# Where the projection's block products stand between the attention's transposes, and how the final rows are grouped for the way out

## The chip, the cores and the metric

The kernel runs on one core of one Trainium2 chip. The metric is the device time of one execution in microseconds (us). Before the change it is 2482.18 us, the median of three runs from 2481.7 to 2482.43 us. The engines are named as in the profile: PE is TensorE's matmul, PEld its weight load, DVE is VectorE, ACT is ScalarE, POOL is GpSimd, SP is SyncE, which issues most DMAs.

## The reference

Two layers of a streaming encoder, for 512 new frames of one stream and 16 frames of each of 8 running streams (640 token columns), with the same weights. Each layer is a half-step SwiGLU block, a mixer and a second half-step SwiGLU block; a last RMSNorm ends it.

```python
for l in range(DEPTH):                                   # DEPTH = 2, D_MODEL = 1024, D_FF = 2816
    x = x + 0.5 * _swiglu(_rmsnorm(x, norm_ffn1[l]), w_ffn1_gu[l], w_ffn1_down[l])
    z = _rmsnorm(x, norm_mix[l]) @ w_in[l]               # conv B, C, V | q | k | v | gates
    y_conv = B * causal_depthwise_conv3(C * V)
    y_attn = chunk_band_attention(q, k, v, rel_bias[l])  # 8 heads x 64, scores + bias, softmax, p @ v
    m = g_conv * (y_conv @ w_conv_out) + g_attn * (y_attn @ w_attn_out)
    x = x + m @ w_o
    x = x + 0.5 * _swiglu(_rmsnorm(x, norm_ffn2[l]), w_ffn2_gu[l], w_ffn2_down[l])
y = _rmsnorm(x, norm_final)
```

All is in float32. The outputs are y, the new k and v rows and the new convolution rows.

## The kernel before

The state x lies in SBUF as `xall`, 128 partitions by 8 row blocks by 640 columns; `x[k]` is one row block. Every operand of a matmul is kept as a high part and a low part (`whi`, `wlo`, `hhim`, `hlom`, `thi`, `tlo`), so a product is three matmuls. Weights come in slabs of 128x1024: SP loads `raw`, ACT makes `whi` of it (L305), DVE makes `wlo` (L310).

**The mixer's products.** A pair of projection blocks is computed by `seven` (L818), a generator that makes seven block products in 14 steps and writes three PSUM tiles, `ma`, `mb` and `mc`. One step is six matmuls of 128x320 (L395). The steps of one product family come in the order X11, X21 (into `ma`, `mb`), N6 (onto `ma`), T5 (into `mc`), T7 (onto `ma`), 22 (onto `mc`), T4 (onto `ma`), two steps each. Between them PSUM tiles are read: ACT copies `ma` after X11 (L836) and after N6 (L844), and `mc` after T5 (L848, into the tile `c`); the product 22 adds onto `mc`, so it may start only when that copy has been made.

**The attention.** `fill(n)` (L1736) takes the next n steps from one stream of such families. Their PE work is laid between the steps of the attention, on which PE would otherwise wait. Two heads make a pair, and each layer has four pairs. For a pair, `scores(p)` computes scores of 128 queries at a time, DVE adds the bias and takes the maximum, ACT does the exponentials (L1969) and the scaling (L1816). `values(p)` then works in three pieces, divided by `yield`. The first piece transposes the weights of the key blocks j = 0 and 1 for both heads on PE (14 transposes, L1829), into four PSUM tiles `ptp`. The second transposes those of j = 2 and 3 (6 transposes). The third is the product with the values (`py`, L1843) and its copy by ACT (L1845). L1832 copies each `ptp` to SBUF (`pt`): DVE does six of a pair's eight, ACT does two, those of the second head with j = 1 and j = 3. The pool `att` has four PSUM banks, so the transposes of the second piece reuse the banks of the first piece, each after its copy.

On PE the order of the program is kept there (`manual_schedule` with PE alone); DVE and ACT are ordered by a scheduler that follows the program's order with some instructions given priority (`soon()`).

**The end.** `Final.all` (L2018) makes the last down projection in two parts of the columns: part A is the first 384 and part B is the last 256. While PE computes part B's row blocks m = 0 to 7, part A's statistics are finished and its rows are scaled and sent: `two(k, rr)` (L2110) multiplies two row blocks of A by their norm on DVE (L2112, 128x768) and SP issues one DMA for them (L2113). This happens after the row blocks m = 5, 6 and 7 of part B, and once more after part B's norm has been made diagonal by `turn(1)`. Then PE spreads part B's norm (`nbcf`, L2103), and `out` (L2115) scales part B's eight row blocks on DVE (L2116), each sent by its own DMA, in turn from SP and ACT (L2118).

Of the kernel before, what the change touches and what calls it, by code (L numbers as in the profile page):

```python
# [13 lines left out]
ALU = mybir.AluOpType  # L14
PSUM = bass.MemoryType.PSUM

P = 128
# [30 lines left out]
PARTS = slice(0, 3 * P), slice(3 * P, T)  # L48
# [132 lines left out]
def trunk(ctx: ExitStack, tc: tile.TileContext, xin, xtok, wst, small, pbias, samplebias, kcache, vcache,  # L181
          yout, ko, vo, co):
    nc = tc.nc
    PE, DVE, ACT, POOL, SP = nc.tensor, nc.vector, nc.scalar, nc.gpsimd, nc.sync
# [21 lines left out]
    def acc(name):  # L206
        return banks["acc"].tile([P, 2, 512], F32, tag="acc", name=name)

    def att(name):
        return banks["att"].tile([P, 512], F32, tag="att", name=name)  # L210
# [15 lines left out]
    for kind, inside in kinds():  # L226
        n = len(fourth)
# [20 lines left out]
    def add(out, a, b):  # L248
        DVE.tensor_tensor(out=out, in0=a, in1=b, op=ALU.add)  # L249
# [58 lines left out]
    def flush():  # L308
        for lo, src, hi in pending:
            DVE.tensor_tensor(out=lo, in0=src, in1=hi.bitcast(F32), op=ALU.subtract)  # L310
        pending.clear()
# [97 lines left out]
    def stir(ps, n):  # L409
        for _ in range(n):  # L410
            PE.matmul(ps[:, :P], ones, ones, start=True, stop=True)
# [4 lines left out]
    xall = xp.tile([P, KT, T], F32, name="x")  # L416
# [75 lines left out]
    def scaled(out, ps, rr):  # L492
        DVE.tensor_tensor(out=halves(out), in0=two(ps), in1=halves(rr), op=ALU.mult)
# [121 lines left out]
    def opening(fp, name, goff, n, put, tails):  # L615
# [45 lines left out]
        def out(i):  # L661

            j, up = divmod(i, 2)
            if not up:
                gs.append(tmp(f"g{name}_{j}"))
                if j:
                    scaled(gs[j], ps[i], ex.rho)
                    ACT.activation(gs[j], gs[j], AF.Silu)
                else:
                    ACT.copy(halves(gs[j]), two(ps[i]))  # L670
                return
            u = tmp(f"u{name}_{j}") if j > 1 else fp.tile([P, T], F32, tag="cap", name=f"u{name}_{j}", bufs=5)
            us.append(u)
            if j:
                scaled(u, ps[i], ex.rho)
                DVE.tensor_tensor(out=u, in0=u, in1=gs[j], op=ALU.mult)
            else:
                ACT.copy(halves(u), two(ps[i]))
# [559 lines left out]
    def mixer(l, after):  # L1238
        with tc.tile_pool(name=f"yp{l}", bufs=1, reuse_waits="tile") as yp, \
# [19 lines left out]
            with tc.tile_pool(name=f"mp{l}", bufs=2, reuse_waits="tile") as mp:  # L1259
# [63 lines left out]
                with tc.manual_schedule(engines={mybir.EngineType.PE}):  # L1323
                    attention(l, h, st, stats, ops, mp, yas, ycp, both, others())
# [374 lines left out]
    def attention(l, h, norms, stats, ops, mp, yas, ycp, both, others):  # L1699


        rr = norms.rr
# [33 lines left out]
        def fill(n):  # L1736
            for _ in range(n):
                next(stream, None)
# [80 lines left out]
        def values(p):  # L1819

            pt = [mp.tile([P, offs[-1] + SEQ], F32, name=f"pt{l}_{2 * p + e}", tag="pt") for e in range(2)]
            at = [sum(P * (NQ - i) for i in range(j)) for j in range(NQ)]

            def turn(j, e):
                w = (NQ - j) * P
                s = weights[2 * p + e]
                ptp = att(f"ptp{l}_{2 * p + e}_{j}")[:, :w]
                for i in range(j, NQ):
                    PE.transpose(ptp[:, (i - j) * P : (i - j + 1) * P],  # L1829
                                 s[:, offs[i] + j * P : offs[i] + (j + 1) * P], ident)  # L1830
                with soon():
                    (ACT.copy if e and j % 2 else DVE.tensor_copy)(pt[e][:, at[j] : at[j] + w], ptp)  # L1832

            for j in range(NQ):
                for e in range(2):
                    turn(j, e)
                if j % 2:
                    yield
            py = att(f"py{l}_{p}")
            for j in range(NQ):  # L1840
                for e in range(2):
                    hh = 2 * p + e
                    PE.matmul(py[e * HD : (e + 1) * HD, j * P :], vs[j][:, hh * HD : (hh + 1) * HD],  # L1843
                              pt[e][:, at[j] : at[j] + (NQ - j) * P], start=j == 0, stop=j == NQ - 1)
            ACT.copy(yas[:, p, 0:SEQ], py)  # L1845
            yield
# [5 lines left out]
        for p in range(npair):  # L1852
            if p + 1 < npair:
                scores(p + 1)
                fill(4)
            vals = values(p)
            next(vals)
            fill(3)
            next(vals)
            fill(2)  # L1860
            next(vals)
            fill(5)


        sbias = mp.tile([P, KS], F32, name=f"sbias{l}", bufs=1)
# [143 lines left out]
    class Final:  # L2009
# [8 lines left out]
        def all(self, ops):  # L2018
            ws = [[tiles.take() for _ in ops] for m in range(KT)]
            flush()  # L2020
            rr = pool[0].tile([P, PARTS[0].stop], F32, tag="even", name="frr", bufs=1)
            A, B = PARTS

            ACT.activation(early, x[KT - 1][:, 0:1], AF.Sqrt, bias=epst[:, 0:1], scale=0.0)
            for m in range(KT):
                self.product(0, m, ops, ws[m])
                self.take(0, m, m < KT - 1)
                if m:
                    self.scale(m - 1)
            for m in range(KT):  # L2030
                self.product(1, m, ops, ws[m])
                if m == 2:
                    self.ps = att("npsf0")[:, : A.stop // P]
                    for b in range(A.stop // P):
                        PE.matmul(self.ps[:, b : b + 1], self.ssum[0][:, b * P : (b + 1) * P], ones[:, 0:1],
                                  start=True, stop=True)
                    self.root(0)
                if m == 3:
                    self.turn(0)
                    self.scale(KT - 1)  # L2040
                if m == 4:
                    ps = self.spread(0)
                if m == 5:
                    self.ps = acc("npsf1")[:, :, 0]
                    self.idle = acc("stirf")[:, 0]
                    self.add(self.ssum[1], True)
                if m > 4:
                    self.add(self.sq)
                if m == 0:
                    last = self.sq  # L2050
                self.take(1, m, m < 4)
                if m == 0:
                    add(self.ssum[0], self.ssum[0], last)
                if m == 4:
                    ACT.copy(rr, ps)
                if m > 4:
                    self.two(2 * m - 10, rr)
            stir(self.idle, 3)
            self.add(self.sq, False, True)
            stir(self.idle, 5)  # L2060
            self.root(1)
            self.turn(1)
            self.two(6, rr)
            ps = self.spread(1)
            for k in range(KT):
                self.out(k, B, ps)
# [40 lines left out]
            xk = x[k][:, PARTS[0]]  # L2107
            ACT.activation(xk, xk, AF.Copy, scale=sm[:, O_GF + k : O_GF + k + 1])

        def two(self, k, rr):  # L2110
            z = xall[:, k : k + 2, PARTS[0]]
            DVE.tensor_tensor(out=z, in0=z, in1=rr.unsqueeze(1).to_broadcast([P, 2, rr.shape[1]]), op=ALU.mult)  # L2112
            SP.dma_start(yout[:, k : k + 2, PARTS[0]], z)  # L2113

        def out(self, k, c, ps):  # L2115
            DVE.scalar_tensor_tensor(out=x[k][:, c], in0=x[k][:, c], scalar=sm[:, O_GF + k : O_GF + k + 1],  # L2116
# [167 lines left out]
```

## Time and profile before

| what | value |
|---|---|
| time, median of three runs | 2482.18 us (2481.7 to 2482.43) |
| the profiled execution's own time | 2482.18 us |
| its span | 2480.2 us |
| PE busy | 2469.0 us, 100% of the span |
| DVE busy | 2119.5 us, 85% |
| ACT busy | 1442.9 us, 58% |
| POOL busy | 361.1 us, 15% |
| granted clock of TensorE | 0.999 |
| moved from and to HBM | 223.75 MB read, 7.94 MB written |

The page gives each engine's busy time, the chain of work that ended last, and groups of instructions. A row of the timeline is start, duration (both us), engine, line, operation, output<-inputs, and in brackets the idle time of that engine just before the instruction and what ended it. A matmul's row is longer than its turn on PE, because matmuls are pipelined: the turn is read from the starts of two rows that follow each other. In the row of a wait the total, the number of times and the longest are given.

### The profile page before, as it was taken

Reading aid. Unit: us, or ns where it says so; the run is one execution under the profiler, and the core shown is the slowest. Engines: PE = TensorE matmul, PEld = TensorE weight load, DVE = VectorE, ACT = ScalarE, POOL = GpSimd, SP = SyncE. Lnnn points to the kernel's source line nnn. Section 1 sums busy time; section 2 is a strip of 40 time slices with the busy share of each in tenths; the row PEclk is TensorE's granted clock in tenths of the full one; section 3 lists DMA queues with packets and bytes.
Section 4 is the critical chain, followed back from the end, with each engine's and each line's share of the span. In section 5 each row is a group of like instructions: output and inputs, shape, how many; then the busy total and the mean of one; then the engine's idle time right before and its main releaser. Section 6 shows DMA issues by size and latency. Waiting matters only on the chain.

```text
span 2480.2 us, 43569 instructions
## 1 busy us (share of the span) xinstructions
PE 2469.0 (100%) x17070; PEld 2422.0 (98%) x17070; DVE 2119.5 (85%) x3344; ACT 1442.9 (58%) x2337; POOL 361.1 (15%) x445
## 2 busy tenths in 40 slices
PE   9999999999999999999999999999999999999998
PEld 9999999889999999999999999998899999999998
DVE  7789888878888899888798889888788888989887
ACT  6445556665666555555565555556656665555555
POOL 0011211210111011111001111221101210111111
PEclk9999999999999999999999999999999999999999
DMA  5245665335345345555435454643344553555554
GB/s 189 82 115 125 136 136 130 107 111 175 104 112 153 95 117 121 133 136 136 117 92 129 129 132 123 138 120 110 122 156 123 119 140 92 122 131 124 129 136 111
DMA packets 134925, 310.72 MB, mean 125 GB/s; under 512 B 12896, under 2 KB 76768, under 8 KB 134720
## 3 DMA queue, kind: packets, MB, share of 16 engines
q1 hardware_dynamic: 70640, 221.80, 27.2%
q0 software_dynamic: 63360, 85.50, 20.7%
q8 instruction: 133, 2.18, 0.4%
q10 hardware_dynamic: 720, 0.65, 0.1%
q14 instruction: 72, 0.59, 0.1%
HBM read 223.75 MB, written 7.94 MB: 93 GB/s over the span
## 4 chain that ended last, share of the span: by engine, by line
PE 96%; ACT 2%; DVE 1%; DMA 0%; issue 0%; DVEq 0%
PE pab L395 12%; PE paa L395 11%; PE pcb L395 6%; PE pca L395 6%; PE dab L1086 5%; PE daa L1086 5%; PE qa L395 4%; PE po L372 4%; PE pbb L395 3%; PE pba L395 3%; PE dcb L1086 3%; PE dca L1086 3%; PE pda L372 2%; PE pv L1752 2%; PE poa L372 2%; PE ma_cv L395 2%
## 5 line engine op out<-in xcount | busy, mean ns | idle before, releaser
L310 DVE TENSOR_TENSOR wlo<-raw,whi 128x1024 fp32r<-128x1024 f32 (+1 forms) x582 | 597.4, 1030 | 243.2 <-ACT whi L305 240.1
L305 ACT CAST whi<-raw 128x1024 fp32r<-128x1024 f32 (+1 forms) x582 | 520.3, 896 | 359.2 <-PE pbb L395 39.4
L305 ACT CAST whi<-s 128x1024 fp32r<-128x1024 f32 (+1 forms) x164 | 153.4, 936 | 243.9 <-issue 109.1
L395 PE MATMUL pab<-xhib,whi 128*128 128x320 f32 x704 | 217.8, 309 | 0.0
L395 PE MATMUL pab<-xlob,whi 128*128 128x320 f32 x704 | 217.4, 309 | 0.0
L395 PE MATMUL pab<-xhib,wlo 128*128 128x320 f32 x704 | 217.4, 309 | 0.0
L395 PE MATMUL paa<-xhia,whi 128*128 128x320 f32 x640 | 197.9, 309 | 0.0
L395 PE MATMUL paa<-xhia,wlo 128*128 128x320 f32 x640 | 197.7, 309 | 0.0
L395 PE MATMUL paa<-xloa,whi 128*128 128x320 f32 x640 | 197.7, 309 | 0.0
L310 DVE TENSOR_TENSOR wlo<-s,whi 128x1024 fp32r<-128x1024 f32 (+1 forms) x164 | 176.3, 1075 | 6.4 <-ACT whi L305 6.1
L395 PEld LDWEIGHTS pab<-xhib,whi 128*128 128x128 f32 x704 | 132.2, 188 | 0.2
L395 PEld LDWEIGHTS pab<-xlob,whi 128*128 128x128 f32 x704 | 132.2, 188 | 0.2
L395 PEld LDWEIGHTS pab<-xhib,wlo 128*128 128x128 f32 x704 | 132.2, 188 | 0.0
L395 PEld LDWEIGHTS paa<-xloa,whi 128*128 128x128 f32 x640 | 120.2, 188 | 0.1
L395 PEld LDWEIGHTS paa<-xhia,whi 128*128 128x128 f32 x640 | 120.2, 188 | 0.1
L395 PEld LDWEIGHTS paa<-xhia,wlo 128*128 128x128 f32 x640 | 120.2, 188 | 0.0
L249 DVE TENSOR_TENSOR raw<-raw,raw 128x512 f32<-128x512 f32 x164 | 112.0, 683 | 1.2
L249 DVE TENSOR_TENSOR raw<-s,raw 128x512 f32<-128x512 f32 x164 | 111.9, 682 | 0.0
L395 PE MATMUL pcb<-xhib,whi 128*128 128x320 f32 x352 | 108.9, 309 | 0.0
L395 PE MATMUL pcb<-xlob,whi 128*128 128x320 f32 x352 | 108.7, 309 | 0.0
L395 PE MATMUL pcb<-xhib,wlo 128*128 128x320 f32 x352 | 108.7, 309 | 0.0
L1110 POOL DMA_DIRECT2D x<-c_b x52 | 62.6, 1203 | 310.4 <-ACT c_b L1103 104.1
(852 smaller groups left out, 8144.9 us busy)
## 6 DMA issues: line engine op xcount, KB each, us to landing
raw<-in_wst SPq DMA_DIRECT2D x374, 512.0 KB, 3.6
x<-c_b POOLq DMA_DIRECT2D x52, 320.0 KB, 5.1
x<-c_a POOLq DMA_DIRECT2D x50, 320.0 KB, 5.0
kc<-in_kcache SPq DMA_DIRECT2D x32, 256.0 KB, 3.7
vc<-in_vcache SPq DMA_DIRECT2D x16, 512.0 KB, 5.5
ub<-cbb POOLq DMA_DIRECT2D x42, 160.0 KB, 5.9
ua<-cba POOLq DMA_DIRECT2D x38, 160.0 KB, 5.5
x<-u_a POOLq DMA_DIRECT2D x18, 320.0 KB, 5.1
```

Of the source, the lines that this page charges most:

```text
L249: DVE.tensor_tensor(out=out, in0=a, in1=b, op=ALU.add)
L305: ACT.copy(hi[:, d], src[:, c])
L310: DVE.tensor_tensor(out=lo, in0=src, in1=hi.bitcast(F32), op=ALU.subtract)
L372: PE.matmul(ps[a] if isinstance(ps, list) else ps[:, a, :HT], w, x[:, a * HT : (a + 1) * HT], start=first and j == 0, stop=last and j == 2)
L395: PE.matmul(ps, a, b, start=start and kp == 0 and j == 0, stop=stop and kp == NP - 1 and j == 2, skip_group_check=True)
L1086: PE.matmul(ps[u], w, y, start=start and i == 0 and j == 0, stop=i == 1 and j == 2, skip_group_check=True)
L1110: POOL.dma_start(rows(r, cols), z, accum_op=ALU.add)
L1752: PE.matmul(pv[t], xx[:, t * P : (t + 1) * P], w[:, kk * AW : (kk + 1) * AW], start=c == 0 and kk == 0 and j == 0, stop=c == KT // 2 - 1 a ...
```

## The change

In the attention, after a pair's first piece of transposes two steps are filled in where there were three, and behind the values six where there were five; two stay between the second transposes and the values. The number of steps for a pair, ten here, is unchanged. At the end, part A's eight row blocks go out in groups of 3, 1, 3 and 1 where they went as four pairs; the number of DMAs stays four.

```diff
             vals = values(p)
             next(vals)
-            fill(3)
+            fill(2)
             next(vals)
             fill(2)
             next(vals)
-            fill(5)
+            fill(6)
...
                 if m > 4:
-                    self.two(2 * m - 10, rr)
+                    self.rows(*((0, 3), (3, 1), (4, 3))[m - 5], rr)
             stir(self.idle, 3)
             self.add(self.sq, False, True)
             stir(self.idle, 5)
             self.root(1)
             self.turn(1)
-            self.two(6, rr)
+            self.rows(7, 1, rr)
             ps = self.spread(1)
...
-        def two(self, k, rr):
-            z = xall[:, k : k + 2, PARTS[0]]
-            DVE.tensor_tensor(out=z, in0=z, in1=rr.unsqueeze(1).to_broadcast([P, 2, rr.shape[1]]), op=ALU.mult)
-            SP.dma_start(yout[:, k : k + 2, PARTS[0]], z)
+        def rows(self, k, n, rr):
+            z = xall[:, k : k + n, PARTS[0]]
+            DVE.tensor_tensor(out=z, in0=z, in1=rr.unsqueeze(1).to_broadcast([P, n, rr.shape[1]]), op=ALU.mult)
+            SP.dma_start(yout[:, k : k + n, PARTS[0]], z)
```

PE's order at the first head pair of the first layer, as the difference of the two programs. `ptp_0_2` is the transpose for head 0 and key block 2; the rows with `mc_qk` ahead of it are the last of the product T5, and those with `ma_qk` are the product T7.

```order
 L395 MATMUL mc_qk_5382<-hhim_6_4655,wlo_5234 128x320
+L1829 MATMUL ptp_0_2_5395<-ident,yc_4689 128x128 x2
+L1829 MATMUL ptp_1_2_5399<-ident,yc_4689 128x128 x2
+L1829 MATMUL ptp_0_3_5403<-ident,yc_4689 128x128
+L1829 MATMUL ptp_1_3_5406<-ident,yc_4689 128x128
 L395 MATMUL ma_qk_5261<-thi_0_4690,whi_5257 128x320
...
 L395 MATMUL ma_qk_5261<-thi_1_4692,wlo_5258 128x320
-L1829 MATMUL ptp_0_2_5408<-ident,yc_4689 128x128 x2
-L1829 MATMUL ptp_1_2_5412<-ident,yc_4689 128x128 x2
-L1829 MATMUL ptp_0_3_5416<-ident,yc_4689 128x128
-L1829 MATMUL ptp_1_3_5419<-ident,yc_4689 128x128
```

The six transposes of the second piece moved from the middle of T7 to its front. The values move in the same way from the middle of the product 22 (which adds onto `mc`) to its front: before, six matmuls of 22 stand ahead of `py`, and now `py` follows the last matmul of T7.

ACT's order at the same place. `whi` is the next slab's high part, `c` is the copy of `mc` after T5, and `pt_1` from `ptp_1_3` is the copy for head 1 and key block 3.

```order
-L305 CAST whi_5398<-raw_5396 128x1024
+L305 CAST whi_5412<-raw_5410 128x1024
 L848 COPY c_4698<-mc_qk_5382 128x320
+L1832 COPY pt_1_5358<-ptp_1_3_5406 128x128
 L1816 ACTIVATE s_2_5277<-s_2_5277,st_2_5278 128x512
-L1832 COPY pt_1_5358<-ptp_1_3_5419 128x128
```

The slab's cast and the copy of `mc` keep their places; the copy for key block 3 moved one instruction ahead. DVE's three copies of the second piece likewise moved ahead of the next slab's L310.

DVE's order at the end, behind part B's row blocks 5, 6 and 7.

```order
 L2078 SCALAR_TENSOR_TENSOR x<-pdf_5_27190,x 128x256
-L2112 TENSOR_TENSOR x<-x,frr 128x2x384
+L2112 TENSOR_TENSOR x<-x,frr 128x3x384
 L2078 SCALAR_TENSOR_TENSOR x<-pdf_6_27208,x 128x256
-L2112 TENSOR_TENSOR x<-x,frr 128x2x384
+L2112 TENSOR_TENSOR x<-x,frr 128x384
 L2078 SCALAR_TENSOR_TENSOR x<-pdf_7_27222,x 128x256
-L2112 TENSOR_TENSOR x<-x,frr 128x2x384
+L2112 TENSOR_TENSOR x<-x,frr 128x3x384
```

The instructions keep their places, and only their widths change; the fourth, after `turn(1)`, is now 128x384 too.

## The prediction

> **What bounds the kernel now.** I read the page first. Its busy times say that PE decides nearly everything:
>
> ```profile
> PE 2469.0 (100%) x17070; PEld 2422.0 (98%) x17070; DVE 2119.5 (85%) x3344; ACT 1442.9 (58%) x2337; POOL 361.1 (15%) x445
> ```
>
> So an edit is worth only what PE loses to waits at the place, and, behind the last matmul, what the last transfers lose. I then asked what PE waits for, longest in total first (total, times, longest):
>
> ```profile
> PE mc_qk L395 <- ACT c L848: 1.6, 4, 0.4
> PE stira L411 <- POOL ones L404: 1.1, 1, 1.1
> PE mc_cv L395 <- ACT c L848: 0.8, 2, 0.4
> PE poa L735 <- DVE whi L650: 0.4, 1, 0.4
> ```
>
> That is the whole list. Six of these waits, the first and the third row, are the product 22 waiting until ACT has copied `mc`. Two layers have four head pairs each, so the wait stands in six of eight pairs. The timeline of PE at the second pair of the first layer shows where (the brackets are idle time by modelled ends, so I read the starts):
>
> ```profile
> 514.73 0.31 PE L395 MATMUL mc_qk<-hhim,wlo 128*128 128x320 f32 x1
> 514.87 0.31 PE L395 MATMUL ma_qk<-thi,whi 128*128 128x320 f32 x1
> ...
> 515.76 0.82 PE L1829 MATMUL ptp<-ident,s 128*128 128x128 f32 x6
> 516.34 0.39 PE L395 MATMUL ma_qk<-thi,whi 128*128 128x320 f32 x1
> ...
> 517.15 0.31 PE L395 MATMUL ma_qk<-thi,wlo 128*128 128x320 f32 x1
> 517.88 0.41 PE L395 MATMUL mc_qk<-hhim,whi 128*128 128x320 f32 x1 [0.42 <-ACT c L848]
> 518.13 0.31 PE L395 MATMUL mc_qk<-hlom,whi 128*128 128x320 f32 x1
> ...
> 518.95 2.38 PE L1843 MATMUL py<-pt,v 128*64 128x512 f32 x16
> ```
>
> In a flowing row the matmuls start 0.14 to 0.15 apart (514.73 to 514.87). From 517.15 to 517.88 are 0.73, and the next start is 0.25 later, because the pipeline fills again. Against 0.15 each, the place loses 0.58 + 0.10 = 0.68 us. ACT's timeline at the same place tells why the copy is late:
>
> ```profile
> 514.99 0.46 ACT L1832 COPY pt<-ptp 128x384 f32<-128x384 f32 x1
> 515.35 0.73 ACT L1816 ACTIVATE yc<-yc,st 128x512 f32<-128x512 f32 x1
> ...
> 516.47 1.04 ACT L305 CAST whi<-raw 128x1024 fp32r<-128x1024 f32 x1
> 517.41 0.42 ACT L848 COPY c<-mc_qk 128x320 f32<-128x320 f32 x1
> ...
> 518.33 0.26 ACT L1832 COPY pt<-ptp 128x128 f32<-128x128 f32 x1
> ```
>
> T5 had been done since about 514.9; ACT came to it at 517.41, behind a scaling, an exponential and a cast, without a pause.
>
> **The first part of the change.** PE gets no more and no fewer instructions. The values `py` now stand between T7 and the product 22. ACT's work ahead of the copy of `mc` is in the same order as before, so the copy still ends near 517.83. PE reaches 22 later: in the new order T5 ends at 514.87, six transposes take 0.58 (515.76 to 516.34), T7's twelve matmuls about 1.8, and `py` 2.38, together 519.6. The copy is then 1.7 us old, and the wait is gone. The refilling after `py` is paid today as well (22's second half follows it now). Six places give 6 x 0.68 = 4.1 us. In the fourth pair of each layer the steps stand at another phase of the family, nothing waits there today, and I count nothing.
>
> What is late next? The second transposes come one step (0.89) earlier, at 514.87 instead of 515.76, and reuse the banks of the first ones. DVE's three copies of those are the other condition, but the latest is ACT's copy of the last one, which starts at 514.99 and ends at 515.45. With 0.05 from a copy's end to PE's start (517.83 to 517.88) the bank is free at 515.50. It is asked for by the fifth of the six transposes, which at 0.1 us each starts near 515.3: a wait of 0.2 us. At the first pair of the layer the rows are closer:
>
> ```profile
> 494.64 0.31 PE L395 MATMUL ma_qk<-thi,whi 128*128 128x320 f32 x1
> 494.65 0.46 ACT L1832 COPY pt<-ptp 128x384 f32<-128x384 f32 x1
> ```
>
> There the transposes would start at 494.64, the fifth near 495.06, and the bank is free at 495.16: 0.1 us. Between 0.1 and 0.2, and 0 to 0.1 for refilling the pipeline after it, I take 0.2 at each of six places, 1.2 us in all; the bounds are 0 (ACT has caught up by then) and 6 x 0.3 = 1.8.
>
> Queued behind that waiting transpose on PE are T7 and all else, so the wait counts in full; ACT and DVE do not wait for it with anything that PE needs soon. `py` needs the copies of the second transposes. DVE makes them right behind those of the first, since they now stand ahead of the next slab's L310, which waits for ACT's cast anyway. ACT's copy for key block 3 now follows the copy of `mc` directly, so it ends about 0.26 after 517.83, at 518.1, and `py`'s last product would need it near 519.4. That cover is 1.3 us; if it went, the excess would be lost at six places. On SP one weight load of each layer now stands behind the two loads of the value cache in the fourth pair; these went out at 551.41 today, and the slab is first read much later:
>
> ```profile
> 551.41 0.94 SPq L1881 DMA_DIRECT2D vc<-in_vcache  x2
> 570.27 1.05 ACT L305 CAST whi<-raw 128x1024 fp32r<-128x1024 f32 x1 [1.18 <-PE mc_b L395]
> ```
>
> Nineteen us cover a load, so this costs nothing. Sum of the part: 4.1 - 1.2 = 2.9 us, between 2.3 and 4.1.
>
> **The second part.** The end of the kernel, from DVE's and PE's timeline, the groups by shape, and the issues:
>
> ```profile
> 2470.27 0.95 DVE L2112 TENSOR_TENSOR x<-x,frr 128x768 f32<-128x768 f32 x1
> 2471.86 0.17 DVE L2098 RECIPROCAL ninvf<-nrmsf 128x2 f32<-128x2 f32 x1 [0.64 <-ACT nrmsf L2093]
> 2472.40 0.95 DVE L2112 TENSOR_TENSOR x<-x,frr 128x768 f32<-128x768 f32 x1
> 2472.58 0.66 PE L2103 MATMUL nbcf<-fsum,ones 128*128 128x256 f32 x2
> 2473.28 3.22 DVE L2116 SCALAR_TENSOR_TENSOR x<-x,sm,nbcf 128x256 f32<-128x256 f32 x8
> L249 DVE TENSOR_TENSOR fsum<-fsum,sqf 128x384 f32<-128x384 f32 x4 | 2.2, 549 | 0.0
> L2113 SPq DMA_DIRECT2D out_yout<-x x4: 372/380/398, 2468.4 to 2473.4; - x4
> L2118 ACTq DMA_DIRECT2D out_yout<-x x4: 338/338/353, 2474.2 to 2476.5; - x4
> ```
>
> A multiplication of 128x384 takes 0.55 (the L249 row), of 128x768 0.95, so each row block adds 0.40. The third group (three blocks) ends at 2470.27 + 1.35 = 2471.62, still ahead of the reciprocal at 2471.86. The last one shrinks to 0.55 and ends at 2472.95; but DVE's next instruction reads `nbcf`, which PE ends at 2473.24, so `out` starts at 2473.28 as before. On DVE the edit is worth nothing, and its cover at the third group is 0.24. What changes is the transfers. Their share of the 16 DMA engines and their rate, in 40 slices of 0.2 us from 2471 to 2479:
>
> ```profile
> DMA  9999958999940000399999999999999999999400
> GB/s 346 369 369 369 338 177 323 369 369 376 384 139 0 0 0 0 131 369 353 369 392 353 323 343 343 333 323 369 328 338 338 338 364 328 343 328 348 159 0 0
> ```
>
> The engines stand still from 2473.4 to 2474.2, start again 0.9 after the issue at 2473.4, and then run full until about 2478.5: 384 KB of A's last pair and 8 x 128 KB of B, 1.44 MB in 4.2 us, 343 GB/s. Now the third DMA carries 576 KB: it starts 0.9 after 2471.62, at 2472.5, and lasts 1.7 until 2474.2; the fourth carries 192 KB and lasts 0.6 until 2474.8; B's 1.05 MB last 3.06, until 2477.85. The last `out` is issued at 2476.5, starts 0.9 later and moves 0.38, so it can't end before 2477.8. The end comes 0.65 us earlier: the pause is filled. Bounds are 0 and 0.7.
>
> The time from issue to landing is the same for A's groups (last column, us) and for B's rows:
>
> ```profile
> out_yout<-x SPq DMA_DIRECT2D x2, 384.0 KB, 2.5
> out_yout<-x SPq DMA_DIRECT2D x4, 128.0 KB, 2.5
> ```
>
> By my reading, the last of B's 2.5 us hold 0.65 of queueing. The Trainium skill, DMA: Bandwidth & Descriptors, section on the anatomy of one DMA, gives about 2.0 us fixed, mostly the write's receipt, plus the bytes at 436 GB/s. By that, an estimate, 128 KB take 2.3 us with no queue at all, and the end would move by some 0.2 at most; the trace shows engines that stand full to the end, which speaks for the queue.
>
> **Sum.** The profiled execution took 2482.18 us, its span 2480.2 and 1.98 around it, and that is also the median of the runs shown. 2.9 + 0.65 = 3.55 us less gives 2478.6. A difference of 0.2% is 5.0 us here, about what a measurement of this kernel can tell from no change.
>
> **The rivals.** *The tail gives nothing*: the landing of 2.5 us is fixed for a DMA of any size here (384 KB and 128 KB land alike); then the last one, issued at 2476.5 as before, lands as before. Against it stand the full slices. The gain is 2.9, the time 2479.3. *The wait only moves*: ACT is still busy at 515.45 without a pause, and if at the earlier transposes it costs about as much as at 22 (0.68, ACT's copy 0.4 later than counted), 0.65 of the tail remains: 2481.5. *Slower*: the same place, but ACT's copy of the first transposes comes 1 us later than its row says, because the cast or an exponential gets in front of it. Then each of six places waits 1.2 us and 0.1 for refilling, 7.8 us against 4.1 + 0.65 won: 2485.2. It decides from a copy 0.6 later than 515.45; the order of ACT shows nothing new ahead of it, which speaks against. *Faster than counted*: the new wait vanishes, the tail gives 0.7, and another 0.2 or more comes from DVE's copies, which now run where DVE idles: 4.1 + 0.7 + 0.2 = 5.0, 2477.2. That the products are not moved at all is excluded by the order.
>
> **How the numbers follow.** The forecast has 0.68, the tail without gain 0.11, the moved wait 0.07, slower 0.05 (0.02 of it beyond 0.2%), more than counted 0.09 (0.08 beyond). The forecast's bounds are 2482.2 - 4.1 - 0.7 = 2477.4 and 2482.2 - 2.3 = 2479.9; 0.4 for the scatter of the runs shown (2481.7 to 2482.43) on the fast side and 0.8 towards the moved wait give 2477.0 to 2480.7. Faster by over 0.2% 0.08, within 0.2% 0.90, slower 0.02.
>
> **What would show it.** Right: the six waits of `mc` on ACT's `c` are gone from PE's list; at the second transposes a short wait on ACT's `pt`, at most 0.3; DMA slices without a pause between the third group and the end, and landings of B's DMAs under 2.0. Wrong: waits of `ptp` on `pt` of 0.5 or more, `py` waiting for `pt`, or B's landings still 2.5 with a pause in front.

## The result and the profile after

The changed kernel takes 2478.70 us (median of 21 runs, 2478.17 to 2480.22), the kernel before 2482.18 us (21 runs beside them, 2481.66 to 2483.23). The ratio is 0.9986, with a 95% interval of 0.9980 to 0.9992: 3.5 us faster, where 3.6 were forecast. The profiled execution took 2478.81 us, its span is 2477.0.

The page's busy times stay as they were; PE is still the bound, and has only lost waiting time:

```profile
PE 2469.1 (100%) x17070; PEld 2422.3 (98%) x17070; DVE 2121.8 (86%) x3344; ACT 1442.6 (58%) x2337; POOL 361.1 (15%) x445
```

PE's list of waits (total, times, longest, in us) has only the one wait at the start of the kernel left:

```profile
PE stira L411 <- POOL ones L404: 1.1, 1, 1.1
```

The ends of matmuls are modelled, so this list misses what is shorter than a pipeline. The weight loads show it. Their list for the kernel before, whose two rows of `mc` sum to 4.1 us:

```profile
PEld mc_qk L395 <- ACT c L848: 2.7, 4, 0.7
...
PEld mc_cv L395 <- ACT c L848: 1.4, 2, 0.7
```

and for the kernel after, where they are gone and the second transposes wait instead:

```profile
PEld ptp L1829 <- ACT pt L1832: 1.5, 6, 0.4
...
PEld aao L1552 <- ACT ya L1559: 0.3, 1, 0.3
```

How much time a stage took is read from two starts of the same instruction. The first transposes (14, L1829) of the first and of the fourth pair frame the three pairs in which the wait stood. PE's timeline before, layer 0 and layer 1:

```profile
491.35 1.69 PE L1829 MATMUL ptp<-ident,yc 128*128 128x128 f32 x14
546.02 1.69 PE L1829 MATMUL ptp<-ident,s 128*128 128x128 f32 x14
...
1718.75 1.69 PE L1829 MATMUL ptp<-ident,yc 128*128 128x128 f32 x14
1773.40 1.69 PE L1829 MATMUL ptp<-ident,s 128*128 128x128 f32 x14
```

and after:

```profile
491.21 1.69 PE L1829 MATMUL ptp<-ident,yc 128*128 128x128 f32 x14
544.56 1.69 PE L1829 MATMUL ptp<-ident,s 128*128 128x128 f32 x14
...
1717.13 1.69 PE L1829 MATMUL ptp<-ident,yc 128*128 128x128 f32 x14
1770.48 1.69 PE L1829 MATMUL ptp<-ident,s 128*128 128x128 f32 x14
```

Layer 0 took 54.67 us between them and takes 53.35; layer 1 took 54.65 and takes 53.35. The mixers gave 1.32 + 1.30 = 2.62 us. At the second pair PE's timeline after reads:

```profile
514.06 0.31 PE L395 MATMUL mc_qk<-hhim,wlo 128*128 128x320 f32 x1
514.21 1.15 PE L1829 MATMUL ptp<-ident,s 128*128 128x128 f32 x6
515.11 0.40 PE L395 MATMUL ma_qk<-thi,whi 128*128 128x320 f32 x1
...
516.82 0.31 PE L395 MATMUL ma_qk<-thi,wlo 128*128 128x320 f32 x1
517.06 2.38 PE L1843 MATMUL py<-pt,v 128*64 128x512 f32 x16
519.36 0.42 PE L395 MATMUL mc_qk<-hhim,whi 128*128 128x320 f32 x1
519.61 0.31 PE L395 MATMUL mc_qk<-hlom,whi 128*128 128x320 f32 x1
```

`py` now stands ahead of the product 22, which follows it without a wait (from 519.36 to 519.61 are 0.25 us, the same refilling as after the wait in the kernel before, 517.88 to 518.13). The six transposes, which took 0.58 from their start to the next product, take 0.90 here (514.21 to 515.11). ACT's timeline at the place tells why:

```profile
513.20 1.31 ACT L1816 ACTIVATE yc<-yc,st 128x128 f32<-128x128 f32 x3
514.41 0.45 ACT L1832 COPY pt<-ptp 128x384 f32<-128x384 f32 x1
...
515.89 1.03 ACT L305 CAST whi<-raw 128x1024 fp32r<-128x1024 f32 x1
516.82 0.41 ACT L848 COPY c<-mc_qk 128x320 f32<-128x320 f32 x1
517.14 0.26 ACT L1832 COPY pt<-ptp 128x128 f32<-128x128 f32 x1
```

The copy of the first transposes ends at 514.86, behind 1.31 us of scaling, and the fifth transpose waits for its bank. (At the first pair of a layer exponentials stand ahead of this copy in place of the scaling.) The copy of `mc` ends at 517.23, 2.1 us before PE needs it.

At the end of the kernel DVE's timeline has the new widths:

```profile
2467.72 1.35 DVE L2112 TENSOR_TENSOR x<-x,frr 128x1152 f32<-128x1152 f32 x1
2469.31 0.17 DVE L2098 RECIPROCAL ninvf<-nrmsf 128x2 f32<-128x2 f32 x1 [0.24 <-ACT nrmsf L2093]
...
2469.86 0.55 DVE L2112 TENSOR_TENSOR x<-x,frr 128x384 f32<-128x384 f32 x1
2470.73 3.22 DVE L2116 SCALAR_TENSOR_TENSOR x<-x,sm,nbcf 128x256 f32<-128x256 f32 x8 [0.32 <-PE nbcf L2103]
```

The share of the 16 DMA engines in 40 slices of 0.2 us from 2468 to 2476, and the median time from issue to landing of the rows of B:

```profile
DMA  9999998000699999999999999999999999994000
...
out_yout<-x SPq DMA_DIRECT2D x4, 128.0 KB, 1.8
```

The pause that is left lies ahead of the third group, at 2469.4 to 2470. From then on the engines do not stand still until the last output, and B's rows land 1.8 us after their issue, where they took 2.5. From the first `out` to the end of the span were 2480.2 - 2473.28 = 6.92 us, and are 2477.0 - 2470.73 = 6.27: 0.65 less.

The span is 3.2 us shorter: 0.14 before the first pair, where nothing was changed, 2.62 in the mixers, 0.16 between the two mixers, 0.65 at the end, and 0.37 were lost between the last mixer and the first `out` (2.92 ahead at 1770.48, 2.55 ahead at 2470.73). Most of this loss is the wait of `aao`, a later product of the second layer, in the list above.

### The profile page after: what moved, and what is told of

Its sections match the earlier page's. It is cut to its first block, busy times and chain, and to the rows that moved or that the text cites. A ratio compares the mean times of both kernels' runs of the same rounds, so it can differ in the third digit from the quotient of the medians.

```text
span 2477.0 us, 43571 instructions
## 1 busy us (share of the span) xinstructions
PE 2469.1 (100%) x17070; PEld 2422.3 (98%) x17070; DVE 2121.8 (86%) x3344; ACT 1442.6 (58%) x2337; POOL 361.1 (15%) x445
## 3 DMA queue, kind: packets, MB, share of 16 engines
q8 instruction: 133, 2.18, 0.4%
## 4 chain that ended last, share of the span: by engine, by line
PE 99%; DVE 1%; ACT 0%; DMA 0%; SPq 0%; issue 0%; DVEq 0%
PE pab L395 13%; PE paa L395 11%; PE pcb L395 6%; PE pca L395 6%; PE daa L1086 5%; PE dab L1086 5%; PE qa L395 4%; PE po L372 4%; PE pbb L395 3%; PE pba L395 3%; PE dcb L1086 3%; PE dca L1086 3%; PE ma_cv L395 2%; PE pda L372 2%; PE pv L1752 2%; PE poa L372 2%
## 5 line engine op out<-in xcount | busy, mean ns | idle before, releaser
L310 DVE TENSOR_TENSOR wlo<-raw,whi 128x1024 fp32r<-128x1024 f32 (+1 forms) x582 | 598.2, 1031 | 234.8 <-ACT whi L305 231.9
L310 DVE TENSOR_TENSOR wlo<-s,whi 128x1024 fp32r<-128x1024 f32 (+1 forms) x164 | 176.6, 1077 | 7.1 <-ACT whi L305 6.7
```

## The experiments

**The steps alone.** The changed numbers of steps, with the rows of the kernel before (`two` as it was there):

```diff
-                    self.rows(*((0, 3), (3, 1), (4, 3))[m - 5], rr)
+                    self.two(2 * m - 10, rr)
...
-            self.rows(7, 1, rr)
+            self.two(6, rr)
```

> Only the steps between the attention's pieces move (2, 2, 6); A's rows go out as four pairs as before. Theory: the mixer's share is the removed wait of the product 22 (6 x 0.68 = 4.1 us) less a new wait of the second transposes on ACT's copy (1.4 us in the trace of the changed kernel), so 2.7 us less than before, about 2479.5; in the profile no wait of mc on ACT's c, the waits of ptp on ACT's pt as in the changed kernel, and the same 0.7 us pause of the DMA engines near the end as before. Rival: the end alone carries the gain and the mixer's is given back later in the stages behind; then 0 to 1 us less than before.

Measured: 2479.66 us (11 runs, 2479.38 to 2480.73) against 2482.16 (33 runs), ratio 0.9990 (0.9981 to 0.9999): 2.5 us less. B's rows land after 2.5 us and the pause in the transfers stands as before. This is the mixers' part.

**The rows alone.** Steps of 3, 2 and 5 as before, groups of 3, 1, 3 and 1.

```diff
-            fill(2)
+            fill(3)
             next(vals)
             fill(2)
             next(vals)
-            fill(6)
+            fill(5)
```

> Only A's rows are grouped 3, 1, 3, 1; the steps stand as before (3, 2, 5). Queue theory: the DMA engines run without a pause from the third group to the end, B's DMAs land 1.8 us after their issue where they took 2.5, and the time is 0.65 us less than before (0.4 to 0.8), about 2481.5. Rival (a landing of fixed length): no change, within 0.2 us of before.

Measured: 2481.36 us (2481.12 to 2482.33) against the same 2482.16, ratio 0.9997 (0.9988 to 1.0005): 0.8 less by the medians, which the interval alone would not tell from nothing. Its profile does: the waits for `c` are those of the kernel before, B's rows land after 1.8 us, and from the first `out` (2473.38) to the end (2479.7) are 6.3. 2.5 + 0.8 = 3.3 us: the two parts add up to the whole within 0.2.

**The transposes early, the values where they were.** Steps of 2, 3 and 5 (as the values stood before), with the new rows. If moving the transposes is what pays, this has the gain.

```diff
             next(vals)
-            fill(2)
+            fill(3)
             next(vals)
-            fill(6)
+            fill(5)
```

> The new grouping of A's rows, and half of the move: the second transposes come one step earlier (2 steps ahead of them), but the step taken away is put between them and the values (2, 3, 5), so that the first half of the product 22 stands ahead of the values as it did before. Theory (it is the place of 22 behind the values that pays): PE still waits for ACT's copy of mc at six places, 0.5 to 0.7 us each, the new wait at the transposes is hidden in that one, and only the end's 0.65 us is left: about 2481.5. Rival (the earlier transposes free the copies and pay by themselves): about as fast as the changed kernel, 2478.7.

Measured: 2481.78 us (2481.16 to 2483.17), ratio 0.9999 (0.9990 to 1.0008). The weight loads' waits in its profile:

```profile
PEld mc_qk L395 <- ACT c L848: 1.9, 4, 0.5
...
PEld ptp L1829 <- ACT pt L1832: 1.4, 6, 0.3
PEld mc_cv L395 <- ACT c L848: 0.9, 2, 0.4
```

1.9 + 0.9 + 1.4 = 4.2 us, where 4.1 stood before: PE waits earlier for ACT, and by as much less at the product 22. The time is 0.4 us less by the medians, less than the end alone gave, so the early transposes alone win nothing; the mixers' gain comes only when `py` stands ahead of 22.

**The values late, the transposes where they were.** Steps of 3, 1 and 6, with the new rows: `py` ahead of 22 as in the change, but the second transposes in the middle of T7 as before.

```diff
-            fill(2)
+            fill(3)
             next(vals)
-            fill(2)
+            fill(1)
             next(vals)
             fill(6)
```

> The new grouping of A's rows, and the other half of the move: the second transposes stay where they were (3 steps ahead of them), and the values come one step earlier (3, 1, 6), so that 22 stands behind the values. Theory: no wait of 22 on ACT's c and no wait of the transposes either, but the values now follow the transposes by one step and DVE's copies of these still stand behind the next slab's low part, which waits for ACT's cast: the values wait about 0.6 us at their key block 2 at six places, so little is won beyond the end's 0.65 us: about 2481 (2480 to 2482). Rival (only the wait of 22 counts): all 4.1 us come and the time is about 2477.4, below the changed kernel.

Measured: 2484.88 us (2484.37 to 2485.72), ratio 1.0011 (1.0002 to 1.0019): 2.7 us slower than the kernel before, though it has the new rows, which alone gave 0.8. About 2481 was expected, some 1 us faster than before; the expectation missed. PE's list of waits has a new first row:

```profile
PE py L1843 <- ACT pt L1832: 7.1, 6, 1.2
```

PE's timeline at the second pair:

```profile
518.77 2.37 PE L1843 MATMUL py<-pt,v 128*64 128x512 f32 x16 [1.18 <-ACT pt L1832]
```

ACT's timeline there:

```profile
516.60 1.04 ACT L305 CAST whi<-raw 128x1024 fp32r<-128x1024 f32 x1
517.54 0.42 ACT L848 COPY c<-mc_qk 128x320 f32<-128x320 f32 x1
517.85 0.63 ACT L1969 ACTIVATE yc<-yc,st 128x384 f32<-128x384 f32 x1
...
518.46 0.26 ACT L1832 COPY pt<-ptp 128x128 f32<-128x128 f32 x1
```

The copy for key block 3 came behind a cast, the copy of `mc` and an exponential, and ended at 518.72. The expectation had put the price on a later matmul of `py` and on DVE. But the trace has `py`'s first weight load wait for ACT here, in the first three pairs of each layer, as it does in the kernel before; in the changed kernel it waits for DVE, and only the 14th of the 16 loads waits for ACT. The first product reads weights that DVE has copied, so the wait for ACT must be for the PSUM bank that `py` is given, that of the transposes for head 1 and key block 3. This is argued from the order; the trace shows the wait and not the bank, and why the bank differs is not shown. In the kernel before it costs nothing, because the copy ends at 518.59 and `py` starts at 518.95. Here the whole of `py` waits, 7.1 us in six places. Neither half of the move is worth anything by itself: the values can stand ahead of 22 without this price only with the transposes a step earlier.

**The groups on DVE, but pairs in the DMAs.** Is it the bytes, or the shorter last multiplication?

```diff
-            SP.dma_start(yout[:, k : k + n, PARTS[0]], z)
+            k -= k % 2
+            SP.dma_start(yout[:, k : k + 2, PARTS[0]], xall[:, k : k + 2, PARTS[0]])
```

> The steps of the changed kernel, and DVE's multiplications of 3, 1, 3 and 1 rows, but each of A's four DMAs still carries a pair of rows (the third one leaves row 6 to the fourth). It asks whether the end came earlier through the bytes that leave early or through the shorter last multiplication. Theory of the bytes: the third DMA of 384 KB starts 0.9 us after its multiplication and lasts 1.13; the fourth is issued behind a multiplication that is 0.40 shorter than in the kernel before, so the pause between them nearly closes, and 1.44 MB at 343 GB/s then still stand ahead of the end: from the first out to the end of the span 6.9 - 0.4 = 6.5 us, where the changed kernel has 6.27 and the kernel before 6.9; time about 2478.9. B's rows land after about 2.1 us. If only the third DMA's size counts: 6.9 again, 2479.4, landings of 2.5. If the shorter multiplication is all: 6.27, 2478.7, landings of 1.8.

Measured: 2479.16 us (2478.65 to 2479.73), ratio 0.9988 (0.9979 to 0.9997), 0.2 to 0.5 above the changed kernel's two medians (2478.70, and 2478.93 below). From the first `out` (2471.02) to the end (2477.6) are 6.58 us, and the landing of B's rows is between those of the other two:

```profile
out_yout<-x SPq DMA_DIRECT2D x4, 128.0 KB, 2.1
```

6.5 and about 2.1 had been expected of the bytes, 6.27 and 1.8 of the multiplication. It is the bytes that stand ahead of B's rows.

**Three, one and four.** Row 7 joins the third group.

```diff
-                    self.rows(*((0, 3), (3, 1), (4, 3))[m - 5], rr)
+                    self.rows(*((0, 3), (3, 1), (4, 4))[m - 5], rr)
...
-            self.rows(7, 1, rr)
```

> The changed kernel with A's rows out as 3, 1, 4: the third group takes row 7 too, and nothing of A is left for the end. DVE's third multiplication grows by 0.40, more than the 0.24 by which it stood ahead of the reciprocal; the reciprocal, and out behind it, come 0.16 later. Theory of the queue (landings of B hold the time in which earlier bytes pass): the third DMA starts 0.40 later and the same 1.82 MB follow at 343 GB/s, so the end is 0.4 later, about 2479.1, with landings of B near 2.0. Rival, that the last out's own issue and a fixed landing of 1.8 set the end: 0.16 later, about 2478.85, landings of 1.8 as now. If DVE's last multiplication had stood on the path, which the forecast excluded: 0.3 earlier, 2478.4.

Measured: 2479.19 us (2478.80 to 2480.22), ratio 0.9988 (0.9979 to 0.9997). DVE's timeline at the end:

```profile
2468.14 1.75 DVE L2111 TENSOR_TENSOR x<-x,frr 128x1536 f32<-128x1536 f32 x1
2469.80 0.16 DVE L2097 RECIPROCAL ninvf<-nrmsf 128x2 f32<-128x2 f32 x1
```

The reciprocal has no wait in front any more: the cover of 0.24 is used up. The landings are 2.1 us, and from the first `out` (2471.21) to the end (2477.9) are 6.69, where the changed kernel has 6.27. That is as the queue has it; a fixed landing would have given 1.8. So a fourth row in the third group costs more than it brings.

**The scaling later.** What remains in the mixers is the wait of the fifth transpose, 0.25 a place. The scaling of the next pair (L1816), which stood ahead of ACT's copy, goes behind the second transposes (`scaling()` runs the list `scales` and empties it):

```diff
-            for i, (o, w) in enumerate(parts):
-                ACT.activation(s[:, o : o + w], s[:, o : o + w], AF.Copy, scale=st[:, 3, i : i + 1])
+
+            def scale():
+                for i, (o, w) in enumerate(parts):
+                    ACT.activation(s[:, o : o + w], s[:, o : o + w], AF.Copy, scale=st[:, 3, i : i + 1])
+
+            scales.append(scale)
...
             next(vals)
             fill(2)
             next(vals)
+            scaling()
             fill(2)
```

> The changed kernel, but in each layer's pairs the scaling of the next pair's softmax (L1816, 0.73 us of ACT) is recorded behind the second transposes instead of ahead of them. Theory: what is left in the mixer is the short wait of the fifth second transpose on ACT's copy of the first transposes, 0.25 a place; where the scaling moves out from ahead of that copy, it comes earlier by what ACT was behind, and the wait goes: 0.2 at each of four places (second and third pairs), 0.8 us less, about 2477.9, and the waits of ptp on ACT's pt in the list of the weight loads go down from six to about two. Rival: ACT is as late by other work (the copies of mc, the casts), the place of the scaling doesn't matter: 2478.7 and six waits as now. Other rival: the scaling then stands ahead of a copy of mc or of the value copies, and values or the next pair's first transposes wait: slower than 2479.

Measured: 2478.50 us (2478.16 to 2479.00), ratio 0.9985 (0.9976 to 0.9994). Only 0.2 less than the changed kernel, where 0.8 was expected, though the mixers gave 0.6 of it. It ran a second time, beside the changed kernel on one chip:

> The changed kernel itself, on the same chip as the next run, as its partner: 2478.7, from the first out to the end of the span 6.27, and no wait of aao on ACT's ya if that wait of 0.3 in its first profile was scatter (by the theory that the change causes it, it is there again).

> The later scaling of the softmax once more. In its first profile the mixer gave 0.61 us over the changed kernel (0.31 in each layer), but 6.87 us passed from the first out to the end, where the changed kernel had 6.27, and its median was only 0.2 lower. Theory: the late end belongs to that one execution, not to the program, whose end is the same; then 6.27 here and a time 0.6 below the partner's. Rival: the end is longer in this program too (a transfer meets something); then 6.8 again and at most 0.2 below the partner.

Measured: the changed kernel 2478.93 us (2478.43 to 2479.61), without the wait of `aao`, which so comes and goes with the execution (the rows alone have it too); the later scaling 2478.28 (2478.02 to 2478.91), 0.65 less by the medians and 0.34 between the two profiled executions (2478.86 and 2478.52). PE's timeline of the later scaling in its second profile:

```profile
491.15 1.69 PE L1838 MATMUL ptp<-ident,yc 128*128 128x128 f32 x14
544.19 1.69 PE L1838 MATMUL ptp<-ident,s 128*128 128x128 f32 x14
```

and the weight loads' waits for the copies:

```profile
PEld ptp L1838 <- ACT pt L1841: 0.6, 4, 0.2
PEld py L1852 <- DVE pt L1841: 0.4, 2, 0.2
```

53.04 us for the three pairs, 0.31 less than in the changed kernel, and 53.04 again in layer 1: 0.62 in all. The wait of the transposes went from 1.5 to 0.6 us, of which 0.4 came back as a wait of `py` for DVE's copies in two places. The waits of the transposes are gone at the third pair, are shorter at the second, and stay at the first, where no scaling stood ahead of the copy. But the end is longer in both of its profiles, 6.87 and 2476.7 - 2469.88 = 6.82 us from the first `out` to the end, where the changed kernel has 6.27 and 6.3 in its two, so the long end is not the chance of one execution. With it the rival's end came true, though not its bound of 0.2 us on the time. Its transfers from 2470 to 2476, in slices of 0.15 us, and the queue of instructions:

```profile
DMA  9999999999999999999999999999930000000000
GB/s 379 358 348 389 389 338 338 410 365 297 348 342 341 348 328 348 335 335 348 362 321 335 321 341 342 321 369 369 369 116 27 20 27 21 0 0 0 0 0 0
...
q14 instruction: 1, 0.01, 0.8%
```

At about 2474.4 the rate falls, and for four more slices 20 to 27 GB/s move, about a sixteenth of the 340 before: by the rate, fifteen engines are done and one is late. The reading is that it also carried the 8 KB of instructions in this stretch; the changed kernel has no row of that queue there. The next runs test it.

**The instructions out of the way.** In the trace's packets the transfer is one of a series about 95 us apart. If the series is ACT's, more instructions on ACT bring it forward:

```diff
-        ACT.copy(early, epst)
+        for _ in range(25):
+            ACT.copy(early, epst)
```

> The later scaling, and 24 more copies of one column on ACT in the first 5 us, where ACT waits 2.3 us for a load. In both profiles of the later scaling one 8 KB transfer on the instruction queue (0.66 and 0.73 us) stands 2.2 us ahead of the last output packet, and one of the 16 DMA engines then finishes its outputs 0.5 us after the others; in the changed kernel the transfer comes 1.9 us behind the last output. It is one of a series about 95 us apart. Theory: the series is ACT's own instructions; 24 more ahead bring the last transfer forward by some 15 us, before the outputs, and the end is as in the changed kernel: from the first out to the end 6.3, time about 2477.8. Rival: another engine's instructions; then the transfer stays where it is, 6.8 again and 2478.3, or later by what the copies cost at the opening.

> The changed kernel with the same 24 copies: the control. If the copies cost nothing at the opening and the last transfer of the series has no part in the changed kernel's end, 2478.7 as before. If the copies delay the opening, as much later as the other padded kernel.

Measured: 2482.10 us (2481.46 to 2483.01) for the later scaling, 2482.81 (2482.28 to 2484.18) for the changed kernel. The copies were mis-costed: 25 of them took 5.54 us, 0.22 each, where ACT's wait of 2.3 us has room for 24 of 0.1, and PE waited 3.2 and 2.8 us for ACT at the opening. But the transfer moved, from 2.2 to 18 us ahead of the last output packet (2472.9 to 2460.3, while the packet before it on that queue only moved with the program, 2447.4 to 2451.5), and the end is short:

```profile
DMA  9999999999999999999999999999970000000000
GB/s 410 369 348 369 399 369 338 338 399 311 348 348 341 341 328 341 342 335 369 314 348 355 321 348 335 335 335 342 362 239 7 0 0 0 0 0 0 0 0 0
```

(slices of 0.15 us from 2474). 2480.1 - 2473.90 = 6.2 us from the first `out` to the end, and the two padded kernels are 0.7 apart. Only ACT got more instructions, so the series is ACT's.

**The same copies where ACT waits.** Behind 24 weight casts of the last feed-forward part:

```diff
             ACT.copy(hi[:, d], src[:, c])
+            if 16 < len(slabs) - i <= 40:
+                ACT.copy(early, hi.bitcast(F32)[:, d.start : d.start + 1])
```

> The later scaling, with the 24 small copies of ACT behind 24 weight casts of the last feed-forward part, where ACT waits 0.7 to 2.2 us before nearly every cast and PE waits for none of them. Theory: the copies cost nothing there, ACT's last instruction transfer comes some 16 us ahead of the last output packet as with the copies at the opening, and the end is as short: from the first out to the end 6.2, time about 2477.7, 1.0 to 1.2 below the changed kernel. Rival: the copies make PE wait (0.1 to 0.2 at some of 24 places), and what the end wins is lost: 2478.3 or more.

Measured: 2477.85 us (2477.66 to 2478.34), ratio to the kernel before 0.9983 (0.9974 to 0.9992). Its `out` begins at 2469.83 and its span ends at 2476.0, 6.2 later. PE waits for none of the copies. The time is 0.85 and 1.1 us below the two medians of the changed kernel, taken on other chips, beside which the kernel before agrees within 0.2.

## Why the prediction was right

*The wait at 22.* Right: six places of 0.68 were 4.1 us, and the weight loads' list of before has 2.7 + 1.4. All six are gone.

*The new wait.* Right in place and cause (the fifth of the six transposes, ACT's copy of the first ones), and taken too small: 0.2 were counted, 1.5 in six is 0.25. The mixers gave 2.62 where 2.9 were forecast, which is this term. That the scaling ahead of that copy makes ACT late at the second and third pairs is shown by the later scaling, which took 0.9 us of this wait away; at the first pair exponentials stand there, and the wait stayed.

*The cover of `py`.* Right in its result, and partly by luck: ACT's copy for key block 3 runs from 517.14 to 517.40, under the 2.3 us of `py`, and nothing waits. The prediction named the order of ACT, in which the copy follows that of `mc` at once, but it took for granted that only the last product of `py` needs this copy. In the kernel before the first one waits for it. Had that stayed so, `py` would have waited from 517.06 to about 517.45 (the end of the copy and 0.05); the same rows at the six places give 0.4 to 0.5 each, by estimate 2.6 us, all that the mixers won. With the values late and the transposes in their old place the first one does wait, and the price was 1.2 us a place.

*The fourth pair, and the load on SP.* Right: neither list has a wait for `c` or `pt` beyond the six places of the first three pairs, or one for the load.

*The end.* Right: `out` follows the reciprocal by 1.42 us before (2471.86 to 2473.28) and after (2469.31 to 2470.73), so DVE's widths are worth nothing, and the filled pause gave 0.65. The two experiments on the groups bear out that the landing held queueing. By the Trainium skill, DMA: Bandwidth & Descriptors, section on the anatomy of one DMA, which writes of DMAs that GpSimd issues, 128 KB would take about 2.3 us with no queue, an estimate. By that rule the end would have moved by 0.2 at most; it moved by 0.65. Here, issued by SP and ACT, they took 1.8, 2.1 and 2.5 us according to what stood ahead, so the measurement decides against a fixed price of 2.0 us on these queues.

*The rivals.* That the tail gives nothing is excluded by the profile of the rows alone. That the wait only moves is what the early transposes alone show, so it was the right rival to a half of the change and wrong for the whole. The slower one was nearer than its chance of 0.05 says: another order at the same place, one step away, gave 2484.9, where the rival had 2485.2. It came through the copy of the second transposes, though, and not of the first.

The step that was mis-sized is the new wait: 1.5 us where 1.2 were counted, so that the mixers and the end together gave 2.62 + 0.65 = 3.27 us and not 3.55. The medians differ by 3.48; the 0.2 between is within what single executions of one kernel scatter (2478.17 to 2480.22), so the agreement of the time to 0.1 us is partly chance.

## What to carry to other kernels

A product that waits for another engine's copy can be moved behind work that is independent of it, but everything that this work needs must move first: here either half of the move was worth nothing or lost 2.7 us, and both together won 2.6. When transfers are the last thing in a kernel, sum the bytes from the last pause to the end, and fill the pause; widths on the computing engine don't matter as long as its own next wait covers them. Ask also which instruction of the moved work waits first, and for what: a bank that is shared can tie its first matmul to a copy that only its last one reads. After an edit that wins less than its stage shows, compare the other stages of the two traces: in both profiles most of a gain of 0.6 us in the mixers was given back at the end, by a transfer that the kernel had not issued.

## What was not expected of the hardware

Instructions come through the same 16 DMA engines as the data, on the queue of ACT's series 8 KB at a time. Where one such transfer (0.66 and 0.73 us long in the two profiles) fell among the last outputs, one DMA engine, by the rate, finished 0.5 to 0.6 us after the other fifteen, and the kernel ended that much later; 24 more instructions on ACT, far ahead of the place, moved it away. The Trainium skill, Runtime: NRT & Kernel Launch, section on instruction fetch mechanics, has each engine refill its instructions through a DMA queue of its own, at a cost that is mostly hidden. The trace agrees that instructions have queues apart from the data's: the page of the changed kernel has two, q14 with 72 packets (0.59 MB, 8 KB each) and q8 with 133 (2.18 MB, 16 KB each). That each engine has one of its own is not shown. This one packet was not hidden, though ACT itself issued its outputs at the usual pace (2470.8 to 2473.1, in the changed kernel 2471.6 to 2474.0). Why the later scaling brought the last transfers of the series 4 to 8 us forward (ACT has as many operations) was not looked into.
